# Splitting the output projection's weights a quarter earlier and reloading them, and loosening the last local attention, in a two-layer decoder trunk

## The chip, the cores and the metric

The kernel runs on one core of a Trainium2 chip (trn2). The metric is device time in microseconds from launch to end; three runs of the kernel before gave a median of 2974.0 us. A difference of less than 0.2%, some 6 us, cannot be told from no change here.

## The reference

The program is a decoder trunk of two layers over 2048 tokens of width 1024, all in float32. Layer A is a gated MLP. Layer B projects queries and a gate `z`, runs three groups of banded attention that share one key/value projection, mixes the groups by softmax of their log-sums, gates, and projects out. Cut to what matters here:

```python
DILATED_GROUPS = ((128, 1), (512, 4), (2048, 16))      # (window, dilation): groups 0, 1, 2
def dilated_layer(x, c, kv_groups, ada_w, ada_b, norm_g, w_in, q_norm_g, w_out):
    shift, scale, gate = ada_mod(c, ada_w, ada_b, 3)
    h = rms_norm(x, norm_g) * (1 + scale) + shift
    qz = h @ w_in
    q, z = ...                                          # 24 heads of 128, then 1024 columns
    for g, (window, d) in enumerate(DILATED_GROUPS):
        o, lse = dilated_group_attn(q[:, :, hs], kb, vb, slopes[hs], window, d)
    alpha = jax.nn.softmax(jnp.stack(lses), axis=0)
    o = jnp.sum(alpha[..., None] * jnp.stack(outs), axis=0)
    y = o.reshape(bsz, s, B_WIDTH) * jax.nn.silu(z)
    return x + gate * (y @ w_out)                       # w_out is b_w_out: 1024 x 1024
```

A large product takes three TensorE passes: each operand is split in a high part, rounded to the fast float32 format, and a low part, the rest. The products are high by high, high by low and low by high. ScalarE makes the high part (a copy) and VectorE the low part (a subtraction).

## The kernel before

**Stages.** The 2048 tokens are worked in four quarters of 512. In each, `layer_A` computes v, u and z of the MLP and its output product; `proj_B` then computes keys and values (`kv_block`), the queries of the three groups (`q_block`) and the gate (`z_block`). A `q_block` or `z_block` is seven products of 24 matmuls (a seven-product scheme on 2 x 2 blocks, `dense_s`). `attend` works an attention group in units of one block of 128 tokens and half of the heads. Each unit has four steps, `att_1` (transposes of keys and queries), `att_2` (scores, maximum, exponentials), `att_3` (transposes of the probabilities) and `att_4` (the product with the values, and the store).

**Fillers.** Side work is written as generators in the list `fillers`. After every few matmuls a dense stage calls `tick`, and `fill` takes the next step of each filler in turn. `rate[0]` says how many steps a tick takes. `drain` runs what is left. All loads and stores go through the SP queue, in order.

**Order on an engine.** A scheduler turns the program into one list for each engine; the engines run their lists strictly in order. A load that waits for its buffer therefore holds all loads behind it on SP.

**Rings.** Buffers come from pools: `rp` (6 raw weight tiles of 128x512), `wp` (8 split weight tiles of high and low part), `xp` (4 tiles of 128x1024; in the last stage the keys and values of a unit are in it), `tp` (8 sums), `ap` (2 of each attention tile, so two of the probabilities `pr`) and `big` (6 tiles of 16 KB on each partition).

**The last stage, `finish`.** It is started ahead of the last quarter's `z_block`. `w_out(0)` and `w_out(1)` are a filler there: 16 loads of `b_w_out` (256 KB each, L1237), each split by ScalarE (L1239) and VectorE (L1240) into four `big` tiles. The filler `first` makes the mixing weights of the first 12 tiles, loads tile 0's two attention outputs and gate with `load(0)` (L1278, L1280; three tiles of `wp`) and combines them (`prepare`). After `z_block`, for each of the 16 token tiles, `make_yb` transposes the gated sum (L1312) and splits it (L1314, L1315), and 2 x 24 matmuls give the output (L1352 to L1354). I call 24 of these matmuls a half. Meanwhile the filler `last` runs the last quarter's local attention (groups 1 and 0 of token blocks 12 to 15, `attend_local`).

**Steps of `attend`.** At iteration i, unit i is in `att_1`, unit i-1 in `att_2` and, with `skew` 1, unit i-2 in `att_3` and unit i-3 in `att_4`. With `skew` 2 the last two come a unit later. Where a stage does not exist yet (the first iterations), the generator yields only if `wrap` is set; without it the first units' steps follow each other with no step between them.

Of the kernel before, what the change touches and what calls it, by code (L numbers as in the profile page):

```python
# [34 lines left out]
def trunk(ctx, tc, out, x, c, a_ada_w, a_ada_b, a_norm_g, a_w_in, a_sgu_g, a_w_spatial,  # L35
# [29 lines left out]
    gd = dp.tile([2, D], F32, name="gd")  # L65
    hd = dp.tile([2, P, KT, 256], F32, name="hd")
# [154 lines left out]
    def ada_gate(w, b, i, nm):  # L221
        for h in range(2):
# [4 lines left out]
            nc.sync.dma_start(row, b[:, 2 * D + h * 512:2 * D + (h + 1) * 512])  # L227
            pg = pst(f"pg_{nm}{h}")
# [149 lines left out]
    flip = [False]  # L378

# [3 lines left out]
    def dense_s(ops, b, nm, evac):  # L383
# [10 lines left out]
        def product(pts, a, w, first):  # L394
# [416 lines left out]
    def layer_A(Q, hA, m, sqv, j0):  # L811
        if Q:
# [100 lines left out]
    def proj_B(Q, hk, hb, keep, rest, ahead):  # L913
# [73 lines left out]
        if Q < NQ - 1:  # L987
            drain()
            ahead()
        q_block(1)  # L990
# [192 lines left out]
    def attend_local(Q, wrap=False):  # L1183

        bs = range(4 * Q, 4 * Q + 4)
        yield from attend([(1, b) for b in bs], wrap, 0, 1 + wrap)
# [4 lines left out]
        yield from attend([(0, b) for b in bs], wrap, 3, 1 + wrap)  # L1191

    def attend(blocks, wrap=False, lead=0, skew=1):


        us = [{"id": (g, b, kh), "wrap": wrap and geom(g, b)[1] == 2, "alt": wrap and kh == 1}
# [12 lines left out]
        for i in range(len(us) + 2 + skew):  # L1209
            for k, st in ((2 + skew, att_4), (1 + skew, att_3), (1, att_2), (0, att_1)):  # L1210
# [7 lines left out]
                elif wrap or i >= len(us):  # L1218
# [11 lines left out]
    def finish():  # L1230
        wo = {}

        def w_out(n):
            wh, wl = wo[n] = [big.tile([P, KT, 512], F32R, tag="big", name=f"wo{n}{i}") for i in range(2)]
            for kk in range(KT):
                raw = rp.tile([P, 512], F32, tag="raw", name=f"rawo{n}{kk}")
                nc.sync.dma_start(raw, b_w_out[kk * P:(kk + 1) * P, n * 512:(n + 1) * 512])  # L1237
                yield
                nc.scalar.activation(wh[:, kk, :], raw, AF.Copy)  # L1239
                nc.vector.tensor_tensor(wl[:, kk, :], raw, wh[:, kk, :].bitcast(F32), ALU.subtract)  # L1240
                yield

# [30 lines left out]
        def load(t):  # L1273
            rw = slice(t * P, (t + 1) * P)
            og = {}
            for g in (0, 2):
                og[g] = wp.tile([P, D], F32, tag="w", name=f"og{t}_{g}")
                nc.sync.dma_start(og[g], od[g][rw, :])  # L1278
            og["z"] = wp.tile([P, D], F32, tag="w", name=f"zt{t}")
# [144 lines left out]
```

## Time and profile before

| what | value |
|---|---|
| median of three runs (lowest, highest) | 2974.0 us (2972.7, 2979.1) |
| profiled execution, its own time | 2975.7 us |
| its span, first to last instruction | 2973.7 us |
| mean granted TensorE clock | 0.997 |
| TensorE (PE) busy | 98% of the span |
| VectorE (DVE), ScalarE (ACT), GpSimd (POOL) busy | 71%, 56%, 25% |
| DMA | 596 MB, 200 GB/s in the mean |
| last quarter's `z_block` | 2641.9 to 2689.6 us |
| local attention and output tiles | 2692 to 2969 us |

In the profile, PE is the matmul engine, PEld the load of its stationary operand, SP the queue that issues the DMAs. A row of the timeline has the start, the time from the first start to the last end, the engine, line, operation, tiles and count; in brackets stands the idle time of the engine ahead of the row and what ended it. A row of the waits has who waited, for whom, the total in us, how often, and the longest. A row of the windows has the stretch and its length, and then the busy time of PE, PEld, DVE, ACT and POOL in it, the granted clock, the DMA engines' busy share and GB/s.

### The profile page before, as it was taken

The numbers are of one execution on the slowest core, as the hardware profiler recorded it, in microseconds if no ns is written. First come the engines' busy times: TensorE is split into PE (matmuls) and PEld (weight loads), VectorE is DVE, ScalarE is ACT, GpSimd is POOL, SyncE is SP. The second block draws the span as 40 slices with busy tenths as digits, with TensorE's granted clock in tenths as the row PEclk, the third lists the DMA queues.
The fourth block names the chain that finished last, engine by engine and source line by source line (L and its number), as shares of the span: only waits on it lengthen the run. The fifth ranks groups of instructions, "written<-read, shape, count | busy, mean of one in ns | idle before, by whom it ended". The sixth has DMA issues, their size and how long they took to land. (4 is left out here: it accounts for less than half of the span.)

```text
span 2973.7 us, 45555 instructions
## 1 busy us (share of the span) xinstructions
PE 2922.2 (98%) x14752; PEld 2446.6 (82%) x14752; DVE 2114.8 (71%) x3794; ACT 1652.1 (56%) x3386; POOL 751.2 (25%) x1044
## 2 busy tenths in 40 slices
PE   7999999999999999999999999999999999999999
PEld 5888788878888888888888888888888888977887
DVE  6877676788556676877758676877668667878772
ACT  4323355766565365776546366675555457867440
POOL 1057002320002313502315214403314220122322
PEclk9999999999999999999999999999999999999999
DMA  8899975886344466884334466873333476788642
GB/s 280 275 306 341 310 237 179 261 301 203 123 125 125 131 196 203 280 271 128 110 115 132 139 196 210 298 243 107 115 117 122 137 228 193 230 285 289 221 162 92
DMA packets 368450, 596.08 MB, mean 200 GB/s; under 512 B 39018, under 2 KB 138572, under 8 KB 368212
## 3 DMA queue, kind: packets, MB, share of 16 engines
q1 hardware_dynamic: 368212, 593.17, 61.8%
q8 instruction: 117, 1.92, 0.3%
q14 instruction: 121, 0.99, 0.1%
HBM read 472.84 MB, written 120.20 MB: 199 GB/s over the span
## 5 line engine op out<-in xcount | busy, mean ns | idle before, releaser
L276 PE MATMUL pd_o<-w_o,yh 128*128 128x512 f32 x1024 | 324.8, 397 | 3.0 <-DVE w_o L248 3.0
L276 PE MATMUL pd_kv<-w_kv,hkh 128*128 128x512 f32 x768 | 239.3, 393 | 0.3
L276 PEld LDWEIGHTS pd_o<-w_o,yh 128*128 128x128 f32 x1024 | 187.7, 189 | 40.8 <-DVE w_o L248 4.2
L314 PE MATMUL pd_u<-hAh,w_u 128*128 128x512 f32 x512 | 208.0, 406 | 0.0
L314 PE MATMUL pd_z<-hAh,w_z 128*128 128x512 f32 x512 | 203.8, 398 | 0.0
L276 PE MATMUL pd_o<-w_o,yl 128*128 128x512 f32 x512 | 200.9, 393 | 0.0
L316 PE MATMUL pd_u<-hAh,w_u 128*128 128x512 f32 x512 | 200.6, 392 | 0.0
L316 PE MATMUL pd_z<-hAh,w_z 128*128 128x512 f32 x512 | 200.1, 391 | 0.0
L315 PE MATMUL pd_u<-hAl,w_u 128*128 128x512 f32 x512 | 199.7, 390 | 0.0
L315 PE MATMUL pd_z<-hAl,w_z 128*128 128x512 f32 x512 | 199.4, 389 | 0.0
L247 ACT ACTIVATE w_u<-raw_u 128x512 fp32r<-128x512 f32 x128 | 79.8, 629 | 166.9 <-PE pd_u L316 93.0
L247 ACT ACTIVATE w_z<-raw_z 128x512 fp32r<-128x512 f32 x128 | 80.3, 631 | 160.0 <-PE pd_z L316 74.5
L276 PEld LDWEIGHTS pd_kv<-w_kv,hkh 128*128 128x128 f32 x768 | 143.2, 189 | 30.7 <-ACT hkh L566 2.0
L248 DVE TENSOR_TENSOR w_z<-raw_z,w_z 128x512 fp32r<-128x512 f32 x128 | 108.2, 853 | 80.9 <-ACT w_z L247 80.4
L1174 PEld LDWEIGHTS po<-kv,pT 128*128 128x128 f32 x1200 | 148.1, 191 | 9.1 <-ACT pT L1019 2.2
L1174 PE MATMUL po<-kv,pT 128*128 128x128 f32 x1200 | 150.6, 275 | 1.2 <-ACT pT L1019 1.2
L247 ACT ACTIVATE w_o<-raw_o 128x512 fp32r<-128x512 f32 x128 | 79.4, 628 | 129.9 <-PE pd_o L276 92.2
L276 PE MATMUL pd_kv<-w_kv,hkl 128*128 128x512 f32 x384 | 149.5, 391 | 0.0
L1113 ACT ACTIVATE pr<-pr,stat,rt 128x256 f32<-128x256 f32 (+1 forms) x224 | 123.0, 551 | 31.1 <-DVE stat L1107 15.5
L248 DVE TENSOR_TENSOR w_o<-raw_o,w_o 128x512 fp32r<-128x512 f32 x128 | 94.7, 749 | 39.5 <-ACT w_o L247 38.2
L248 DVE TENSOR_TENSOR w_u<-raw_u,w_u 128x512 fp32r<-128x512 f32 x128 | 94.0, 749 | 34.0 <-ACT w_u L247 32.1
L248 DVE TENSOR_TENSOR w_q<-raw_q,w_q 128x512 fp32r<-128x512 f32 x144 | 96.9, 693 | 24.0 <-ACT w_q L247 22.9
(826 smaller groups left out, 8030.3 us busy)
## 6 DMA issues: line engine op xcount, KB each, us to landing
raw_q<-in_b_w_in_dram SPq DMA_DIRECT2D x144, 256.0 KB, 3.6
raw_u<-in_a_w_in_dram SPq DMA_DIRECT2D x128, 256.0 KB, 3.7
raw_z<-in_a_w_in_dram SPq DMA_DIRECT2D x128, 256.0 KB, 2.9
raw_o<-in_a_w_out_dram SPq DMA_DIRECT2D x128, 256.0 KB, 3.1
qt<-qd SPq DMA_DIRECT2D x96, 260.0 KB, 3.1
raw_v<-in_a_w_in_dram SPq DMA_DIRECT2D x96, 256.0 KB, 4.2
raw_kv<-in_w_kv_dram SPq DMA_DIRECT2D x96, 256.0 KB, 2.9
od<-ot SPq DMA_DIRECT2D x96, 256.0 KB, 2.7
```

The lines of the kernel that those rows point to most:

```text
L247: nc.scalar.activation(hi, src, AF.Copy)
L248: nc.vector.tensor_tensor(lo, src, hi.bitcast(F32), ALU.subtract)
L276: last_mm[0] = nc.tensor.matmul(pt, a, u[:, w, :], start=f, stop=e, skip_group_check=more)
L314: nc.tensor.matmul(pts[i], wh, hh[:, k, :], start=k == 0, stop=False)
L315: nc.tensor.matmul(pts[i], wh, hl[:, k, :], start=False, stop=False)
L316: nc.tensor.matmul(pts[i], wl, hh[:, k, :], start=False, stop=k == KT - 1)
L1113: nc.scalar.activation(pr[:, i, :], pr[:, i, :], AF.Exp, bias=mneg[:, i:i + 1], scale=u["rt"][:, h:h + 1], accum_out=lsum[:, i:i + 1])
L1174: nc.tensor.matmul(po[:, h * P:(h + 1) * P], u["pT"][h // hp][:, h % hp, j, :], u["kv"][:, j, kh, 1, :], start=j == 0, stop=j == nk - 1)
```

## The change

It has five parts.

1. **Split earlier.** A new filler, `presplit`, runs in `layer_A` of the third quarter (`Q == 2`), whose rate goes from 2.2 to 2.6. It loads the 16 tiles of `b_w_out`, splits them in `wp` tiles and stores both parts (512 KB each) in a new DRAM tensor `wod`.
2. **Reload.** In the last quarter `load_wo` loads eight pieces of 1 MB from `wod` into four `big` tiles, from a list `jobs` that is worked off one entry at the end of each product of `dense_s`: four in `q_block(1)` and `q_block(0)`, four in the last three products of `z_block`. The filler `w_out` is gone, and the rate in `z_block` falls from 4.8 to 2.0.
3. **Last local attention.** It has `skew` 2 instead of 1, and the probabilities of every second unit are in `tp` (`alt`), as the wrapped attentions had them. The rate is 5.0 instead of 4.9.
4. **Empty first steps.** `attend` now always yields where a stage does not exist yet; this holds for group 2's attention in the last quarter too, whose rate stays 9.2.
5. **Small ones.** Tile 0's three loads go to `xp` instead of `wp`; `ada_gate` yields twice more ahead of its matmul.

```diff
+    def presplit():
+        us, raws = {}, {}
+        for i in range(2 * KT + 2):
+            if i >= 2:
+                nc.sync.dma_start(wod[(i - 2) // KT, (i - 2) % KT], us.pop(i - 2).bitcast(F32))
+            if i < 2 * KT:
+                n, kk = divmod(i, KT)
+                raws[i] = rp.tile([P, 512], F32, tag="raw", name=f"rawo{n}{kk}")
+                nc.sync.dma_start(raws[i], b_w_out[kk * P:(kk + 1) * P, n * 512:(n + 1) * 512])
+            if 1 <= i <= 2 * KT:
+                us[i - 1] = wp.tile([P, 2, 512], F32R, tag="w", name=f"wos{i - 1}")
+                split(us[i - 1][:, 0, :], us[i - 1][:, 1, :], raws.pop(i - 1))
+            yield
+
+    def load_wo(n, q):
+        if q % 2 == 0:
+            wo[n, q // 2] = big.tile([P, 4, 2, 512], F32R, tag="big", name=f"wo{n}{q // 2}")
+        h = q % 2 * 2
+        nc.sync.dma_start(wo[n, q // 2][:, h:h + 2].bitcast(F32), wod[n, 2 * q:2 * q + 2].rearrange("k p t c -> p k t c"))
...
+            job = jobs.pop(0) if jobs else None
+            if job:
+                with tc.issue_after(last_ld[0].ins):
+                    job()
...
-            rate[0] = 2.45 if Q == 1 else 2.2
+            rate[0] = 2.45 if Q == 1 else 2.6 if Q == 2 else 2.2
...
+            if Q == 2:
+                fillers.append(presplit())
...
+        if Q == NQ - 1:
+            for n in range(2):
+                jobs.extend([None] * 2 + [lambda n=n: load_wo(0, 2 * n), None, None, lambda n=n: load_wo(0, 2 * n + 1), None])
+            jobs.extend([None] * 4 + [lambda: (load_wo(1, 0), load_wo(1, 1)), lambda: load_wo(1, 2),
+                                      lambda: load_wo(1, 3)])
...
-        yield from attend([(1, b) for b in bs], wrap, 0, 1 + wrap)
+        yield from attend([(1, b) for b in bs], wrap, 0, 1 + (wrap or alt), wrap or alt)
...
-        yield from attend([(0, b) for b in bs], wrap, 3, 1 + wrap)
+        yield from attend([(0, b) for b in bs], wrap, 3, 1 + (wrap or alt), wrap or alt)
...
-                elif wrap or i >= len(us):
+                else:
                     yield
...
+            pool, tag = (wp, "w") if t else (xp, "xin")
...
-            yield from attend_local(NQ - 1)
+            yield from attend_local(NQ - 1, False, True)
...
-        fillers.extend([fs, both()])
-        rate[0] = 4.8
+        fillers.append(fs)
+        rate[0] = 2.0
...
-        rate[0] = 4.9
+        rate[0] = 5.0
```

No matmul, VectorE or GpSimd instruction is added or taken away over the whole program, and ScalarE loses seven table loads. What is new are the 16 stores and the 8 reloads. The rest is order.

**SP in the last three products of the last `z_block`.** `raw_z3bt` from `wt_0` are the weights of the fifth product, those from `wt_3` of the sixth, `raw_z3b` those of the seventh; `rawo` is a piece of `b_w_out`, `wo` a reload, `zd` a store of the gate. Before:

```order
L255 DMA raw_z3bt_3_26126<-wt_0_116 128x512
L960 DMA qd_92<-st_q30u_25254 128x520
...
L1237 DMA rawo_26140<-in_b_w_out_dram 128x512
L1237 DMA rawo_26158<-in_b_w_out_dram 128x512
...
L255 DMA raw_z3bt_0_26179<-wt_3_119 128x512
...
L969 DMA zd<-zb_2_26172 128x512
L255 DMA raw_z3bt_3_26194<-wt_3_119 128x512
...
L1237 DMA rawo_26212<-in_b_w_out_dram 128x512
...
L255 DMA raw_z3b_0_26243<-in_b_w_in_dram 128x512
...
L255 DMA raw_z3b_3_26258<-in_b_w_in_dram 128x512
L1237 DMA rawo_26268<-in_b_w_out_dram 128x512
...
L969 DMA zd<-zb_2_26236 128x512
```

After:

```order
L258 DMA raw_z3bt_3_26201<-wt_0_117 128x512
...
L258 DMA raw_z3bt_0_26243<-wt_3_120 128x512
...
L258 DMA raw_z3bt_3_26258<-wt_3_120 128x512
L403 DMA wo_26231<-wod 128x2x1024
L1000 DMA zd<-zb_0_26118 128x512
...
L403 DMA wo_26231<-wod 128x2x1024
L403 DMA wo_26286<-wod 128x2x1024
L258 DMA raw_z3b_0_26299<-in_b_w_in_dram 128x512
L1000 DMA zd<-zb_2_26236 128x512
...
L258 DMA raw_z3b_1_26304<-in_b_w_in_dram 128x512
...
L258 DMA raw_z3b_3_26314<-in_b_w_in_dram 128x512
L403 DMA wo_26286<-wod 128x2x1024
```

The weights of the fifth and sixth product now stand ahead of any gate store; three reloads of 1 MB and two pairs of gate stores stand ahead of the seventh product's last three pieces.

**PE at the start of the last local attention.** `pyb` are the transposes of tile 0, `pf` its output, `pk` and `pq` the transposes of `att_1`, `ps` the scores of `att_2`, `pp` the transposes of `att_3`. Before, with only some of the output matmuls shown:

```order
L1312 MATMUL pyb_0_26317<-ident,og_0_25973 128x128 x4
...
L1050 MATMUL pk_12_26370<-ident,kv_12_26363 128x128 x4
L1352 MATMUL pf_0_26356<-wo_25883,yb_26316 128x512
...
L1060 MATMUL pq_12_0_26378<-ident,qt_12_0_26366 128x128 x4
L1352 MATMUL pf_1_26497<-wo_26156,yb_26316 128x512
...
L1098 MATMUL ps_12_00_26391<-kT_12_26375,qT_12_0_26383 128x256
```

After:

```order
L1337 MATMUL pyb_0_26358<-ident,og_0_26094 128x128 x4
...
L1086 MATMUL pk_12_26420<-ident,kv_12_26401 128x128 x3
L1373 MATMUL pf_0_26397<-wo_24371,yb_26357 128x512
...
L1096 MATMUL pq_12_0_26428<-ident,qt_12_0_26404 128x128 x2
...
L1373 MATMUL pf_1_26453<-wo_26231,yb_26357 128x512
...
L1337 MATMUL pyb_0_26455<-ident,og_0_26351 128x128 x4
...
L1134 MATMUL ps_12_00_26492<-kT_12_26425,qT_12_0_26433 128x256
```

Between the first unit's `pq` and its `ps` stood 16 output matmuls before; now its scores come in the second half, behind the rest of the first half and the transposes of tile 1 (the second `pyb`), and its `pp` follow in the fourth half instead of the second. The last `po` (the `att_4` product) of the local attention moves from half 16 of 32 to half 20.

More of the change, by code (lines that the diff above doesn't have):

```diff
@@ L65, in trunk @@
     gd = dp.tile([2, D], F32, name="gd")
+    wod = dp.tile([2, KT, P, 2, 512], F32, name="wod")
     hd = dp.tile([2, P, KT, 256], F32, name="hd")
@@ L227, in ada_gate @@
             nc.sync.dma_start(row, b[:, 2 * D + h * 512:2 * D + (h + 1) * 512])
+            yield
+            yield
             pg = pst(f"pg_{nm}{h}")
@@ L1230, in finish @@
     def finish():
[L1231 to L1241, printed above, removed]
         gb = [bcast(gd[1:2, n * 512:(n + 1) * 512], f"gb{n}") for n in range(2)]
@@ L1317, in finish @@
         fs = first()
-        def both():
-            yield from w_out(0)
-            yield from w_out(1)
-        fillers.extend([fs, both()])
-        rate[0] = 4.8
+        fillers.append(fs)
+        rate[0] = 2.0
         yield
```

20 lines of the change are left out of this document (11 added, 9 removed).

## The prediction

> **What bounds the kernel now.** I read the page's first part, then TensorE's waits by stretch of time, then the windows of those stretches.
>
> ```profile
> span 2973.7 us, 45555 instructions
> PE 2922.2 (98%) x14752; PEld 2446.6 (82%) x14752; DVE 2114.8 (71%) x3794; ACT 1652.1 (56%) x3386; POOL 751.2 (25%) x1044
> ```
>
> PE is busy for all but 51.5 us of its span. The change adds and removes no matmul, so it can win no more than the part of these idle times, and of the slow matmuls beside them, that lies where it reorders. The waits of PE in three stretches (group 2's attention in the last quarter; the last `z_block`; the output tiles) say where that is:
>
> ```profile
> PE pp L1155 <- ACT pr L1113: 3.1, 1, 3.1
> PE po L1174 <- ACT pT L1019: 1.2, 2, 0.7
> PE pq L1060 <- DMA qt<-qd: 1.2, 1, 1.2
> PE pp L1155 <- DVE b_s L1103: 0.5, 1, 0.5
> PE pk L1050 <- DVE pr L1103: 0.4, 1, 0.4
> ...
> PE pd_z3bb L276 <- DVE w_z3b L248: 2.1, 2, 1.2
> PE pd_z3ba L276 <- ACT w_z3bt L247: 1.8, 1, 1.8
> PE pf L1352 <- ACT yb L1314: 1.3, 1, 1.3
> ...
> PE pp L1155 <- ACT pr L1113: 3.8, 3, 1.4
> PE ps L1098 <- ACT qT L1065: 2.9, 1, 2.9
> PE pyb L1312 <- DVE pT L1017: 0.3, 1, 0.3
> ```
>
> In `z_block` PE waits for split weights, in the attentions for probabilities. The windows give what each stretch loses; the fourth is the `z_block` of the quarter before, which has no `b_w_out` beside it:
>
> ```profile
> 100.00:400.00 300.00, 297.24 (x1396) 248.69 (x1395) 214.01 (x276) 100.39 (x179) 101.92 (x72) 0.99 0.93 311
> 1357.00:1434.00 77.00, 77.00 (x434) 66.59 (x433) 54.62 (x108) 42.74 (x84) 23.53 (x37) 1.00 0.36 112
> 1890.30:1931.30 41.00, 41.00 (x193) 33.88 (x192) 33.30 (x50) 24.10 (x41) 16.96 (x22) 1.00 0.89 303
> 2450.00:2470.00 20.00, 15.55 (x82) 12.30 (x81) 8.02 (x25) 8.24 (x24) 3.33 (x7) 0.91 0.44 142
> 2465.00:2642.00 177.00, 174.49 (x1141) 155.14 (x1142) 141.89 (x359) 147.48 (x413) 26.46 (x55) 0.99 0.74 231
> 2641.90:2689.60 47.70, 41.73 (x169) 32.11 (x168) 34.91 (x54) 29.29 (x53) 8.81 (x15) 0.96 0.87 293
> 2780.00:2800.00 20.00, 17.10 (x85) 14.57 (x84) 10.05 (x19) 5.45 (x14) 4.93 (x3) 0.91 0.79 268
> 2692.00:2880.00 188.00, 180.39 (x1138) 157.69 (x1139) 151.49 (x304) 107.69 (x306) 58.92 (x36) 0.99 0.64 217
> ```
>
> **The change part by part.** I sum against the profiled execution's own 2975.7 us.
>
> *The last `z_block`.* Two products of the timeline, one behind the other, give the length of an undisturbed one:
>
> ```profile
> 2636.46 5.60 PE L276 MATMUL pd_q30a<-w_q,hob 128*128 128x512 f32 x24
> 2641.90 5.60 PE L276 MATMUL pd_z3bb<-w_z3b,hob 128*128 128x512 f32 x24
> ```
>
> Starts are 5.44 us apart, so seven products need 38.1; this `z_block` took 47.7 and lost 9.6. What goes away is 16 loads in the six raw tiles that the z weights use too, and their splits:
>
> ```profile
> L1239 ACT ACTIVATE wo<-rawo x16: 614/631/634, 2637.3 to 2690.7; 128x512 fp32r<-128x512 f32 x16
> L1240 DVE TENSOR_TENSOR wo<-rawo,wo x16: 677/685/693, 2640.9 to 2691.3; 128x512 fp32r<-128x512 f32 x16
> DMA to landing us min/median/max: 3.7/4.6/5.5
> ```
>
> That is 10 us of ACT and 11 of DVE. The z weights get the six raw tiles for themselves, and wp too, since tile 0 now lies in xp. That such a block can run without loss at 303 GB/s the window 1890 to 1931 shows. What stays is the seventh product. The reloads wait on SP until PE is done with the third and fourth product (their `big` tiles hold its operands), and behind them stand gate stores and the seventh product's weights, then tile 1's loads. Three reloads of 1.05 MB at this window's 293 GB/s take 10.7 us; from the third product's end to the seventh's start are 3 x 5.44 = 16.3; the 5.6 left are a load's landing (4.6) and one pair of splits (1.3), just too few. The seventh product waited before too:
>
> ```profile
> 2684.48 5.28 PE L276 MATMUL pd_z3bb<-w_z3b,hob 128*128 128x512 f32 x22 [0.93 <-DVE w_z3b L248]
> ```
>
> Now its third piece stands on ACT behind the sixth's two gate activations. I leave 1.6 us lost: **-8.0**, between -9.6 and -2.6 (all four pieces late, by a landing and splits).
>
> *First output matmul.* ACT came to `yb` behind the last `b_w_out` splits, and PE waited 1.3. One gate activation still stands ahead of each half of `yb`, at about the 0.63 us of the copy above: **-0.7** (0 to -1.3). What is late next is tile 1: its gate load stands on SP behind the last gate stores. From the seventh product's end these need two sums (0.7 each) and two activations (0.6), then a landing of 4.6 and POOL's product of 2.4 (its row stands below), 9.6 us; PE has the first half and four matmuls, 6.3, the transposes and the wait ahead of them, 2: **+1** (0 to +3).
>
> *Last local attention.* PE lost 7.0 us in waits, and 20 x (1 - 0.91) = 1.8 us by the slower clock behind the longest (the window from 2780). `ps` gets most of a half more cover behind `pq`, against 2.9 us of wait; `pp` gets a whole unit's work more behind its exponentials, against waits of 1.4 at most. DVE's work there (151 us of 188) is the same, over four more halves. Its `pr` in `tp` adds two buffers to the two that had to come free. Some first-unit waits will stay: **-6.0** (0 to -8.8; a loss is left to the rivals).
>
> *Group 2's attention* gets the same empty steps. PE lost 6.4 us in waits (the first five rows; 0.7 of it in the last units) and 1.8 us of clock (window from 2450). The 1.2 for `qt` should go, since the second unit's `pq` comes 12 kv matmuls behind the first's instead of 4. The way from the scores to the probabilities was 8.5 us, from the end of
>
> ```profile
> 2455.34 1.16 PE L1094 MATMUL ps<-kT,qT 128*128 128x128 f32 x8
> ```
>
> to 2465.0, and PE had 5.4 us of work or waits in between; the new order puts 18 kv matmuls (5.44 / 24 = 0.227 us each, 4.1) and some 2 us of transposes and scores there. 2 us of waits stay and half of the clock: **-3.5** (0 to -7.5).
>
> The clock is seen in the rows of the two longest waits:
>
> ```profile
> 2465.01 0.95 PE L1155 MATMUL pp<-ident,pr 128*128 128x128 f32 x2 [3.10 <-ACT pr L1113]
> 2465.62 1.20 PE L276 MATMUL pd_kv<-w_kv,hkh 128*128 128x512 f32 x2
> 2793.18 0.58 PE L1098 MATMUL ps<-kT,qT 128*128 128x256 f32 x1 [2.90 <-ACT qT L1065]
> 2793.56 0.41 PE L1099 MATMUL ps<-kT,qT 128*128 128x256 f32 x1
> ```
>
> Two matmuls of 512 columns take 1.20 us behind the wait of 3.10. [...]
>
> *Price in the q-blocks.* Four reloads of 1.05 MB stand on SP between query loads. VectorE runs in order and already waits there:
>
> ```profile
> DVE rt L1070 <- DMA qt<-qd: 18.9, 17, 3.1
> ```
>
> With 141.9 busy of 177 it has 16 us left over. Four reloads hold what is behind them by up to 1.05 / 293 = 3.6 us each, 14 in all, so the slack would just bear it: **+2** (0 to +8, half of it passed on).
>
> *Price in the third quarter.* 16 x (0.26 + 0.52) MB more over the first 36 filler steps; at 2.6 steps a tick, with two ticks to a block of 48 matmuls (10.9 us), that is some 76 us and 166 GB/s on top of 112, 278 in all. From 100 to 400 us PE kept 99% at 311 GB/s. ACT and DVE get 10 and 11 us in 77, where they were busy for 43 and 55, while attention steps are halved for that time. A split product pair there lasts 12 x 0.227 = 2.7 us; with three wp tiles lent out five remain, 13.6 us ahead, three landings. **+1** (0 to +28, the rival below).
>
> *`ada_gate`.* This wait in the first quarter goes, and the steps behind it shift a little: **-0.6**.
>
> ```profile
> PE pg_ga L229 <- DVE acc_ga L178: 0.8, 1, 0.8
> ```
>
> *End of the local attention.* It moves from half 16 to 20 of 32, towards tile 12, which needs its result. From the last sums to the end of a tile's product on POOL the chain was 10.3 us, and a tile lasts 11.77:
>
> ```profile
> 2867.78 1.23 DVE L1170 TENSOR_TENSOR stat<-stat,stat 128x4 f32<-128x4 f32 x1
> 2875.72 2.41 POOL L1290 TENSOR_TENSOR og<-og,zt 128x1024 f32<-128x1024 f32 x1 [6.73 <-PE pf L1354]
> 2940.06 1.09 ACT L1314 ACTIVATE yb<-pyb 128x512 fp32r<-128x512 f32 x2 [10.69 <-PE pyb L1312]
> 2951.83 1.09 ACT L1314 ACTIVATE yb<-pyb 128x512 fp32r<-128x512 f32 x2 [10.69 <-PE pyb L1312]
> ```
>
> Half 24, where tile 12 is transposed, begins three halves (17 us) behind half 20. Cost 0; with the chain twice as long it would be 3 us.
>
> Sum: -8.0 - 0.7 + 1 - 6.0 - 3.5 + 2 + 1 - 0.6 = -14.8, to 2960.9. The profiled execution was 1.7 us above the median, so **2959 us** as a median; its own range is 2953 to 2966.
>
> **Rivals.**
>
> - *All of it goes.* For: the other `z_block` has no loss. Against: first units always wait for something. 9.6 + 1.3 + 8.8 + 7.5 + 0.8 = 28.0 less: 2946.
> - *The reloads starve the seventh product and the query loads.* 293 GB/s speak for it, the z weights now standing ahead of the reloads against. `z_block` wins 2.6 and the q-blocks lose 5 where I have 8.0 and 2: 8.4 more, 2967.
> - *The waits for probabilities stay*, since VectorE sets the chain's pace, and its work stays:
>
> ```profile
> 2692.00:2740.00 48.00, 45.94 (x300) 40.41 (x301) 44.60 (x78) 38.24 (x107) 18.35 (x8) 1.00 0.85 294
> ```
>
> 93% busy speaks for it; against it that fewer units now stand in these halves. Local attention wins 1.0, group 2's nothing: 8.5 more, 2968.
> - *Slower: the loss of the `z_block` moves to the third quarter and grows.* The same 16 loads share the same six raw tiles, now with 16 stores of twice the size that wait on SP for their split, ahead of the u weights. In `z_block` a load cost 9.6 / 16 = 0.6 us; with the stores at 1.2 it is 16 x 1.8 = 28.8, less the 1 I have: 2987. It decides once a u weight lands later than the 13.6 us for which split tiles are there. Against: 4.6 us of landing at 293 GB/s.
> - *No net change*, where half of the gains are kept and 8 us are paid: 2974.
>
> **Chances.** Forecast 0.45, all gone 0.08, reloads starve 0.15, waits stay 0.12, slower 0.12, none 0.08. A median within 0.2% (6 us, 2968 to 2980) is no change that a measurement can tell. Of the two middling rivals, at the bound, a third falls there, so faster is 0.45 + 0.08 + 0.10 + 0.08 = 0.71, no change 0.17, slower 0.12. The range reaches up to 2974, which leaves out the slower case and half of none, and down to 2948, which leaves out most of the first rival.
>
> **What would show it.** In the new profile: no wait of PE for z weights but in the seventh product, and `z_block` within 40 us; one wait under 1 us at the first output matmul; less than 3 us of waits from there on, and no window at 0.91; in the third quarter's u stretch PE still at 100% with some 270 GB/s; query waits of VectorE above 19 us but none of PE. I am wrong if PE waits for u weights, if it waits for `wo`, or if tile 12's transposes wait for POOL.

## The result and the profile after

The changed kernel is slower. Nine runs gave a median of 2982.9 us (2981.6 to 2989.4), nine of the kernel before 2975.7 (2971.0 to 2979.1). The ratio of the runs is 1.0033, with a 95% interval of 1.0024 to 1.0043: 7 to 13 us more, some 9.8 of 2974. The prediction said 2959. One profiled execution of the experiments below, that of e14, ran at a granted clock of 0.66 and took 4186 us, so for e14 there is the ratio of its other runs and no stage lengths.

The profiled execution took 2982.0 us, 6.3 more than that of before. The first part of its page:

```profile
span 2979.8 us, 45570 instructions
PE 2921.9 (98%) x14752; PEld 2448.6 (82%) x14752; DVE 2115.6 (71%) x3794; ACT 1643.3 (55%) x3379; POOL 757.2 (25%) x1044
```

Every engine is as busy as before. PE stood idle for 57.9 us instead of 51.5. So the question is again where it waits. I cut both timelines of PE at the first matmul of a stage (the first that writes the named tile) and compared the lengths:

| stage (from, to) | before, us | change, us | predicted, us |
|---|---|---|---|
| start to the first quarter's queries (`pd_q02a`) | 461.4 | +5.1 | -0.6 |
| second quarter, `layer_A` and keys (`pd_v1a` to `pd_q12a`) | 462.8 | +1.5 | 0 |
| third quarter, the same (`pd_v2a` to `pd_q22a`) | 473.2 | +4.1 | +1 |
| last quarter, the same (`pd_v3a` to `pd_q32a`) | 473.3 | +1.7 | 0 |
| last query blocks with group 2 (`pd_q32a` to `pd_z3bb`) | 237.3 | 0.0 | -3.5 + 2 |
| last `z_block`, to the first `pf` | 50.5 | -10.1 | -8.0 - 0.7 |
| output tiles, first to last `pf` | 275.8 | +3.8 | +1 - 6.0 |

The other stages (query and gate products of the first three quarters, 178.0 us each) are the same to 0.1. The terms add up to the 6.1 us between the spans. The gain in `z_block` is there and larger than forecast. It is eaten by stages that the prediction had at about nothing.

The waits of PE name what stands there. First the kernel before, between 300 and 700 us:

```profile
PE pd_o L276 <- DVE w_o L248: 2.8, 1, 2.8
...
PE pt_b L560 <- DVE xr L893: 0.5, 1, 0.5
```

The kernel after, in the same stretch:

```profile
PE pt_b L589 <- DVE xr L924: 5.4, 1, 5.4
...
```

The kernel after from 2460 to 2700 us (group 2 and `z_block`), and from 2692 (the output tiles):

```profile
PE pq L1096 <- DMA qt<-qd: 3.8, 1, 3.8
...
PE pd_z3bb L279 <- DVE w_z3b L251: 0.2, 1, 0.2
...
PE ps L1134 <- DVE yb L1340: 2.7, 2, 1.7
PE pyb L1337 <- POOL og L1315: 2.1, 1, 2.1
PE ps L1136 <- DVE qT L1102: 2.0, 2, 1.1
PE pf L1375 <- DVE yb L1340: 1.8, 1, 1.8
PE ps L1134 <- DVE kT L1092: 1.4, 1, 1.4
...
```

All waits of `pp` for `pr` are gone, as forecast: 3.1 us in group 2 and 3.8 in the output tiles. In group 2 a wait of 3.8 for a query load stands in their place. In the output tiles it is VectorE's queue, with 7.9 us, and tile 1's gate, with 2.1.

**The first quarter.** The two `yield`s in `ada_gate` push all later steps of its side work. SP's rows of the kernel before:

```profile
390.39 0.32 SPq L360 DMA_DIRECT2D wt<-st_cw  x1
...
403.77 0.93 SPq L890 DMA_DIRECT2D x1d<-xr  x2
```

Its last store of combined weights (`wt`) goes out at 390.4. The kernel after, the rows of SP, VectorE and PE:

```profile
392.72 8.21 SPq L363 DMA_DIRECT2D wt<-st_cw  x8
401.02 3.66 SPq L258 DMA_DIRECT2D raw_kv<-in_w_kv_dram  x6
404.77 0.85 SPq L921 DMA_DIRECT2D x1d<-xr  x2
411.52 0.75 DVE L924 TENSOR_SCALAR xr<-xr,r_b 128x1024 f32<-128x1024 f32 x1 [2.46 <-DMA x1d<-xr]
412.42 1.09 PE L589 MATMUL pt_b<-ident,xr 128*128 128x128 f32 x4 [5.37 <-DVE xr L924]
```

Now eight such stores (256 KB each) and six loads of key weights stand right ahead of the store of the rows `xr`. VectorE may scale these rows in place only when that store has read them. It does so 6.8 us after the store's issue at 404.8; in the kernel before it was 3.1 us (403.77 to 406.83). PE, which transposes the rows next, waits 5.4 us.

**The third quarter.** Its `u` stretch, where `presplit` loads and stores, costs nothing: PE 77.00 of 77 us at 259 GB/s. The loss lies in the output product, two stages later. Windows of the kernel after, the `u` stretch and two of the output product (columns as in the prediction):

```profile
1363.00:1440.00 77.00, 77.00 (x410) 66.00 (x409) 54.67 (x98) 42.08 (x80) 12.94 (x20) 1.00 0.77 259
...
1600.00:1657.00 57.00, 55.77 (x324) 47.90 (x324) 50.28 (x118) 24.54 (x65) 34.24 (x42) 1.00 0.47 148
1657.00:1718.00 61.00, 59.56 (x311) 49.59 (x310) 39.47 (x80) 22.32 (x52) 18.23 (x24) 1.00 0.45 143
```

The same two of the kernel before:

```profile
1593.00:1650.00 57.00, 57.00 (x324) 49.09 (x323) 47.08 (x106) 29.52 (x66) 28.28 (x37) 1.00 0.40 125
1650.00:1707.00 57.00, 57.00 (x291) 47.83 (x290) 33.94 (x64) 18.96 (x42) 13.02 (x17) 1.00 0.50 160
```

In `u` GpSimd, which works for the attention, has 12.9 us instead of 23.5 (the prediction shows that window). In the output product GpSimd and VectorE have 11 and 9 us more than before, in windows that are 4 us longer. Some of the attention that `presplit` displaced runs there, beside the splits of `w_o`.

### The profile page after: what moved, and what is told of

It is laid out like the page before. It is cut to its first block, busy times and chain, and to the rows that moved or that the text cites. A ratio compares the mean times of both kernels' runs of the same rounds, so it can differ in the third digit from the quotient of the medians.

```text
span 2979.8 us, 45570 instructions
## 1 busy us (share of the span) xinstructions
PE 2921.9 (98%) x14752; PEld 2448.6 (82%) x14752; DVE 2115.6 (71%) x3794; ACT 1643.3 (55%) x3379; POOL 757.2 (25%) x1044
## 5 line engine op out<-in xcount | busy, mean ns | idle before, releaser
L1149 ACT ACTIVATE pr<-pr,stat,rt 128x256 f32<-128x256 f32 (+1 forms) x192 | 104.2, 545 | 40.1 <-DVE stat L1143 23.4
L250 ACT ACTIVATE w_q<-raw_q 128x512 fp32r<-128x512 f32 x144 | 88.6, 626 | 46.8 <-PE pd_kv L279 11.2
```

The costliest lines, as they stand in the source:

```text
L250: nc.scalar.activation(hi, src, AF.Copy)
L1149: nc.scalar.activation(pr[:, i, :], pr[:, i, :], AF.Exp, bias=mneg[:, i:i + 1], scale=u["rt"][:, h:h + 1], accum_out=lsum[:, i:i + 1])
```

## The experiments

Each kernel was timed in five rounds beside the kernel before. The columns behind the ratio are the stage lengths of its profiled execution against those of before, as above: the first quarter, the third quarter, the last quarter's `layer_A`, group 2, `z_block`, output tiles.

| run | ratio | interval | 1st | 3rd | last A | grp 2 | z | tiles |
|---|---|---|---|---|---|---|---|---|
| the change | 1.0033 | 1.0024–1.0043 | +5.1 | +4.1 | +1.7 | 0.0 | -10.1 | +3.8 |
| e1 yields alone | 1.0023 | 1.0014–1.0032 | +4.5 | -0.9 | -0.3 | -1.1 | +3.2 | -1.1 |
| e2 change, no yields | 1.0007 | 0.9997–1.0017 | -3.0 | +4.8 | +2.1 | +0.9 | -9.9 | +9.7 |
| e3 change, old local attention | 1.0043 | 1.0031–1.0056 | +2.5 | +4.9 | +2.5 | +0.9 | -10.1 | +6.1 |
| e4 change, old group 2 | 1.0040 | 1.0025–1.0054 | +4.2 | +5.2 | +2.5 | +1.1 | -8.4 | +4.4 |
| e5 split, reload, xp | 1.0010 | 0.9999–1.0021 | +0.5 | +4.2 | +1.6 | -0.8 | -7.2 | +3.2 |
| e6 both attentions alone | 0.9997 | 0.9988–1.0006 | -3.0 | -0.4 | -0.2 | +1.3 | -1.1 | +1.4 |
| e7 e2, tile 0 in wp | 1.0036 | 1.0023–1.0049 | -2.8 | +3.3 | +1.0 | -0.2 | +1.8 | +0.5 |
| e8 presplit alone | 1.0034 | 1.0020–1.0047 | -0.9 | +7.0 | +2.3 | +0.3 | +1.1 | +2.6 |
| e9 tile 0 in xp alone | 0.9991 | 0.9982–1.0001 | -1.5 | +1.8 | +0.5 | +1.0 | -3.3 | +1.3 |
| e10 e9 and attentions | 0.9995 | 0.9984–1.0005 | -2.9 | +0.7 | 0.0 | -2.6 | -0.7 | +0.9 |
| e11 e2, rate 3.8 | 0.9990 | 0.9979–1.0001 | -1.4 | +2.9 | -0.3 | +4.1 | -8.7 | +6.4 |
| e12 e2, tile rate 4.4 | 0.9992 | 0.9981–1.0003 | -0.3 | +7.6 | +1.0 | -0.4 | -9.6 | +1.2 |
| e13 e11 and e12 | 0.9981 | 0.9973–0.9990 | -2.9 | +2.2 | -0.5 | +0.6 | -9.0 | +1.5 |
| e14 e13, tile rate 4.0 | 0.9979 | 0.9969–0.9989 | | | | | | |
| e15 e13, old group 2 | 0.9977 | 0.9968–0.9986 | -2.4 | +2.2 | -0.2 | +2.6 | -6.5 | -2.7 |
| e16 e13, old local attention | 0.9989 | 0.9978–0.9999 | -0.6 | +3.5 | -0.1 | +1.1 | -8.6 | +3.9 |
| e17 e2, gate on VectorE | 0.9999 | 0.9988–1.0010 | -2.0 | +8.8 | +1.7 | +0.1 | -3.2 | -7.3 |
| e18 e15, gate on VectorE | 0.9968 | 0.9955–0.9980 | -2.4 | +3.7 | -0.1 | +1.8 | -8.7 | -5.3 |

Stage lengths are of one execution each. The first quarter has the same steps in all kernels without the yields, and there they lie between -3.0 and +0.5; so a single difference under some 3 us says little, a column that repeats says more. A profiled execution need not be a typical one either: that of e2 took 4.5 us more than the median of e2's runs and that of e11 7.7 more, that of e7 7.8 less and that of e13 4.6 less. Where the ratio and the stage lengths disagree, the ratio decides.

**The yields (e1, e2).** Alone in the kernel before, and taken out of the change:

```diff
             nc.sync.dma_start(row, b[:, 2 * D + h * 512:2 * D + (h + 1) * 512])
+            yield
+            yield
             pg = pst(f"pg_{nm}{h}")
```

> The kernel before, with only the two added yields in ada_gate. Theory A (the profile after shows 5.4 us of PE waiting for the scaled rows in the first quarter, behind weight stores that came some 7 us later): the yields alone cost 4 to 7 us, 2980 to 2982 where the kernel before has 2975, and the wait of pt_b for xr near 412 us stands in this profile too. Rival B (the wait is scatter of one execution, or comes from elsewhere in the change): within 2 us of the kernel before, pt_b waits under 1.5 us in all up to 1280 us.

> The changed kernel without the two yields in ada_gate. Theory A: 5 to 7 us less than the changed kernel, 2976 to 2978, and kv_block(0) of the first quarter starts where it did in the kernel before (415 us). Rival B: no change, 2983.

Alone they cost 0.23%, 6.8 us. Without them the change goes from 1.0033 to 1.0007, 7.7 us less, and the two intervals don't touch. Neither leaves room for the -0.6 of the prediction. The mechanism is in e1's rows, the same as in the kernel after:

```profile
391.98 8.62 SPq L362 DMA_DIRECT2D wt<-st_cw  x8
...
403.59 0.86 SPq L892 DMA_DIRECT2D x1d<-xr  x2
...
410.95 1.09 PE L562 MATMUL pt_b<-ident,xr 128*128 128x128 f32 x4 [5.26 <-DVE xr L895]
```

In the three profiles of the change with yields (the kernel after, e3, e4) this wait was 5.4, 4.7 and 5.7 us; in e2 it was 0.5.

**The orders of the attentions (e3, e4, e6).** e3 takes the new order out of the last local attention (with its old rate 4.9), e4 takes the empty first steps out of group 2, e6 puts both attentions' parts alone into the kernel before. The edit of e3 in part; `pad` is a new argument, false for an attention without the empty steps:

```diff
-            yield from attend_local(NQ - 1, False, True)
+            yield from attend_local(NQ - 1)
...
-                else:
+                elif pad or wrap or i >= len(us):
                     yield
```

> The changed kernel with the last local attention as before (skew 1, no probabilities in tp, no empty first steps there, rate 4.9); group 2 keeps its empty steps. Theory A (the new order of the local attention itself costs time, since its transposed keys and queries now stand behind the split of yb on VectorE): 3 to 6 us less than the changed kernel, 2977 to 2980, with waits of pp for pr again and none of ps for yb. Rival B (the tail is long because tile 1 comes late and VectorE is held beside GpSimd, whatever the order): within 1.5 us of the changed kernel. The prediction's own reason (the new order saves 6 us): 6 us more, 2989.

> The changed kernel without the empty first steps in group 2's attention; the local attention keeps its own. Theory A (a wait for the query load took the place of the wait for probabilities): within 1.5 us of the changed kernel, 2982 to 2984, with a wait of pp for pr of some 3 us and none for qt over 2 us. The prediction's reason (the empty steps save 3.5 us): 2 to 5 us more. Rival (the empty steps bring the third query load behind the stores of the keys and values and so cost more than they save): 2 to 4 us less.

> The kernel before with the new order of the attentions alone: skew 2, probabilities in tp and rate 5.0 in the last local attention, empty first steps in both; b_w_out is loaded and split in the last z_block as before. The prediction's terms (-6.0 - 3.5): 7 to 10 us less than the kernel before. Theory A (the local attention wins 3 us as e3 told, group 2 wins 0 to 2): 3 to 5 us less. Rival B (the waits of the output tiles for yb and qT come with this order, whatever the z_block does): 0 to 4 us more, with ps waiting for yb in this profile.

e3 is 0.10% above the change, some 3 us, and e4 0.07%, some 2, each with intervals that overlap. e6 is 0.9997 (-3.6 to +1.8 us): the 9.5 us that the prediction gave to the two orders aren't there. My theory that the new local order itself costs time fell with e3, which is not faster. In e3 the old waits of `pp` for `pr` are back (7.4 us, 2.5 twice), beside one of 1.35 for `yb`: each order has its own kind of wait. In e6 `ps` waits 3.9 us for `yb`, so that wait comes with the new order, with or without the reload. For group 2 the trace of the kernel after shows what came in the place of the wait for probabilities:

```profile
2466.70 0.32 SPq L1075 DMA_DIRECT2D qt<-qd  x1
2472.84 2.25 SPq L956 DMA_DIRECT2D kvd<-hs_k  x4
2475.18 0.45 SPq L1075 DMA_DIRECT2D qt<-qd  x1
...
2478.55 1.09 PE L1096 MATMUL pq<-ident,qt 128*128 128x128 f32 x4 [3.79 <-DMA qt<-qd]
```

The third unit's query load stands on SP behind the stores of the normalised keys (`kvd`), which wait for VectorE until 2472.8. The kernel after asks for that load with the third unit's step, but PE reaches this step before the stores are out. All eleven profiles with the empty steps in group 2 have one such wait for `qt`, 3.0 to 4.1 us, and none of `pp` for `pr`. Of the eight without them five have the wait of 3.1 for `pr`; e4, e5 and e8 have neither, at about the same length of the stage (+1.1, -0.8, +0.3).

**What of the z_block's gain is whose (e5, e7, e9, e10).** e5 has only the split, the reload, tile 0 in `xp` and the rates. e7 is e2 with tile 0 in `wp`; e9 is the kernel before with tile 0 in `xp`; e10 adds both attentions to e9. The edit of e9:

```diff
         def load(t):
+            pool, tag = (wp, "w") if t else (xp, "xin")
...
-                og[g] = wp.tile([P, D], F32, tag="w", name=f"og{t}_{g}")
+                og[g] = pool.tile([P, D], F32, tag=tag, name=f"og{t}_{g}")
...
```

> The changed kernel without the two yields and with both attentions as before: what is left of the change is the split in the third quarter, the reload, tile 0 in xp and the rates 2.6 and 2.0. Theory A (the z_block's gain of some 10 us is kept, 4 us go in the third quarter, 2 in the last quarter's layer A and 6 in the output tiles): within 0.1% of the kernel before, 2970 to 2975 where that has 2972. Rival B (the output tiles lose time by the new order of the attention alone): 4 to 7 us less than the kernel before. The prediction's own terms (-8.0 - 0.7 + 1 + 2 + 1): 5 us less.

> The changed kernel without the two yields and with tile 0's three loads in wp as before. Theory A (what the output tiles lose comes from tile 1's late gate and from VectorE, not from xp): z_block loses 2 to 5 us more by the three wp tiles, the output tiles stay within 1.5 us of e2; 2 to 5 us more than e2. Rival B (tile 0 in xp keeps the keys of the local attention waiting and costs the output tiles 4 us or more): 2 to 4 us less than e2.

> The kernel before with one edit: tile 0's three loads go to xp instead of wp. Theory A (e7 showed that with tile 0 in wp the z_block loses all again, so the three wp tiles and not the loads of b_w_out were what it lost by): the z_block takes 5 to 10 us less, the output tiles give 2 to 4 back, 2 to 7 us less in all. Rival B (the 16 loads and splits of b_w_out in the raw tiles were the loss, as the prediction said): z_block within 2 us, total within 2 us.

> The kernel before with tile 0 in xp and the new order of both attentions; no split a quarter earlier, no reload, no yields. Theory A: as e9, with the output tiles 0 to 2 us better or worse, 2 to 7 us less than the kernel before. Rival B (what the z_block wins the output tiles lose, since VectorE sets their pace): z_block 5 to 10 us less, output tiles 5 to 10 us more, within 2 us of the kernel before.

Neither part does it alone. The reload without `xp` leaves the `z_block` at +1.8 (e7), `xp` without the reload at -3.3 and -0.7 (e9, e10); with both it is -6.5 to -10.1 in eleven of the twelve profiles (e17, with the gate's product moved too, is the other, -3.2). In time e7 lies 0.29% above e2, 8.6 us, for one line on tile 0. Both theories of e9 were too simple. Not all that `z_block` wins stays won: e7's output tiles took 9 us less than e2's in these profiles, and why is not traced. The rows of e7 show why the reload alone doesn't help:

```profile
2659.45 0.43 SPq L401 DMA_DIRECT2D wo<-wod  x1
...
2661.76 0.87 SPq L401 DMA_DIRECT2D wo<-wod  x1
2662.73 3.77 SPq L256 DMA_DIRECT2D raw_z3bt<-wt  x4
...
2674.51 5.72 PE L277 MATMUL pd_z3ba<-w_z3bt,hob 128*128 128x512 f32 x14 [5.56 <-ACT w_z3bt L248]
```

With three split tiles lent to tile 0, the sixth product's weights come behind two reloads of 1 MB on SP, and PE waits 5.6 us. In the kernel after they stand ahead of the reloads, as the front part's rows show, and the window of its whole `z_block` has only 0.2 us without work at 349 GB/s:

```profile
2654.30:2693.30 39.00, 38.77 (x170) 31.26 (x169) 27.39 (x41) 22.07 (x41) 9.13 (x14) 1.00 0.98 349
```

**The third quarter (e8, e11).** e8 is the kernel before with `presplit` and its rate; it stores weights that nothing reads. e11 is e2 with a higher rate while `presplit` runs:

```diff
-            rate[0] = 2.45 if Q == 1 else 2.6 if Q == 2 else 2.2
+            rate[0] = 2.45 if Q == 1 else 3.8 if Q == 2 else 2.2
...
             yield
+        rate[0] = 2.2
```

> The kernel before with the 16 loads, splits and stores of presplit and the rate 2.6 added in the third quarter; the stored weights are never read, b_w_out is loaded and split again in the last z_block. Theory A: 4 to 6 us more than the kernel before, of which 3.5 to 5 between the third quarter's v and its first query block and 1.5 to 2.5 in the last quarter's layer A. The prediction's term: 1 us more. Rival (the loss of the z_block moves here whole): 28 us more.

> The changed kernel without the yields (e2), with rate 3.8 while presplit runs and 2.2 behind it, so that the attention beside it loses 3 steps instead of 12 and is not pushed into the output product of the third quarter. Theory A (the 4 us of the third quarter are attention work that moved beside the splits of w_o): 2 to 4 us less than e2 there, and w_o waits under 1 us. Rival B (the loads and stores themselves, 350 GB/s then): PE waits for u weights and the third quarter takes 2 us or more longer than in e2.

`presplit` alone costs 0.34%, 10 us, in time; its profile has 9.3 of it in the third quarter and the last quarter's `layer_A`, 2.8 of these in the `v` product, ahead of `presplit`. Over all nine profiles with the rate 2.6 the third quarter lost 3.3 to 8.8, over the four without `presplit` -0.9 to +1.8, over the five with 3.8 then 2.2 it lost 2.2 to 3.7. From the first `u` matmul on, where `presplit` begins, the three groups stand clear of each other: 4.2 to 6.5, 0.0 to 0.5, and 1.5 to 2.2. The last quarter's `layer_A` lost 1.0 to 2.5 with 2.6 and nothing with 3.8. In time e11 is 0.17% below e2, with intervals that just overlap. The waits in the third quarter's output product of the kernel after, between 1590 and 1720 us:

```profile
PE pd_o L279 <- DVE w_o L251: 1.2, 2, 1.1
...
```

and of e13, which has the rate 3.8 too:

```profile
PE pd_o L277 <- DVE w_o L249: 0.3, 1, 0.3
```

The transfers are the same at both rates, so more than half of the price in the third quarter comes from the attention steps that `presplit` took the place of, and not from the transfers. PE's waits in these 130 us come to 2.6 of the 4.1 us, 1.4 of them for split weights; the rest of it, the 1.5 to 2.2 us that stay at rate 3.8, and the loss in the last quarter are not traced.

**The output tiles (e12 to e16).** e12 to e14 change one number, the rate over the output tiles, e12 on top of e2, e13 and e14 on top of e11. e15 and e16 are e13 with group 2, or the last local attention, in its old order. The edit of e12:

```diff
-        rate[0] = 5.0
+        rate[0] = 4.4
```

> The changed kernel without the yields (e2), with rate 4.4 instead of 5.0 over the output tiles. Theory A (VectorE and its sharing with GpSimd set the pace of the first 20 halves): spreading the same work over 23 halves makes the waits of ps for yb, kT and qT smaller, 2 to 5 us less than e2. Rival B (tile 1's late gate and single late loads): within 1.5 us of e2. Rival C (the local attention then ends too late for tile 12): 3 us or more longer.

> The changed kernel without the yields, with rate 3.8 beside presplit (as e11) and 4.4 over the output tiles (as e12). Theory A (two separate prices, each from work pushed too densely into one stretch): the gains add, 0.2 to 0.35% less than the kernel before, 2965 to 2969 where that has 2974; the output tiles within 3 us of the kernel before. Rival B (e11 and e12 are scatter around e2): 0 to 0.1% more than the kernel before.

> As e13, but with rate 4.0 over the output tiles, so that the local attention is spread over some 25 halves. Theory A (density on VectorE makes the waits): the waits of PE between the first output matmul and half 20 fall again, but the attention ends at tile 12; within 2 us of e13 or up to 3 us less. Rival C (tile 12 then waits for it): 2 to 6 us more than e13, with one wait of pyb near 2880 us. Rival B (single late loads): within 1 us of e13.

> As e13, without the empty first steps in group 2's attention. Theory A (a wait for the query load took the place of that for probabilities, nothing won): within 2 us of e13, with the wait of pq for qt under 2.5 us. The prediction's reason: 2 to 5 us more than e13. Rival (the third query load behind the stores of keys and values costs more than the empty steps save): 2 to 4 us less.

> As e13, with the last local attention in the old order (skew 1, no probabilities in tp, no empty steps there) at the same rate 4.4. Theory A (the new order saves some 2 to 3 us of waits for probabilities as e3 told): 2 to 4 us more than e13. The prediction's reason: 6 us more. Rival B (density alone decides): within 1.5 us of e13.

With 4.4 the output tiles took 1.2 us more than before (e12) where e2's took 9.7 more. PE's waits for VectorE there fell from 8.7 us (e2) to 4.2 (e12). e12 is 0.15% under e2 in time and e13 0.09% under e11; each pair overlaps, but both go one way, and so do the stage lengths. e13 is the first kernel clearly faster than that before, 0.9981. e14 adds nothing and loses nothing: tile 12 did not come to wait by a measurable amount. e15 equals e13 within its interval (0.9977 against 0.9981): group 2's empty steps are worth nothing that can be measured, either way. e16 lies 0.08% above e13, with intervals that overlap: if the new local order is worth anything it is some 2 us, a third of the 6 forecast.

**What holds VectorE (e17, e18).** In the output tiles of the kernel after some of VectorE's instructions take much longer than their like. Rows of VectorE, GpSimd and PE:

```profile
2719.47 3.31 POOL L1315 TENSOR_TENSOR og<-og,zt 128x1024 f32<-128x1024 f32 x1 [3.92 <-DVE stat L1143]
2720.63 3.23 DVE L1314 TENSOR_TENSOR og<-og,og 128x1024 f32<-128x1024 f32 x1
2724.00 2.36 POOL L1315 TENSOR_TENSOR og<-og,zt 128x1024 f32<-128x1024 f32 x1 [1.22 <-DMA xr<-x1d]
2724.99 1.41 DVE L1106 COPY rt<-qt 128x8 f32<-128x8 f32 x1
2725.21 0.35 PE L1134 MATMUL ps<-kT,qT 128*128 128x256 f32 x1 [1.40 <-DVE kT L1092]
...
2751.79 2.37 POOL L1315 TENSOR_TENSOR og<-og,zt 128x1024 f32<-128x1024 f32 x1 [6.00 <-DVE stat L1143]
2752.16 2.03 DVE L1106 COPY rt<-qt 128x8 f32<-128x8 f32 x1
2754.84 0.38 PE L1134 MATMUL ps<-kT,qT 128*128 128x256 f32 x1 [1.72 <-DVE yb L1340]
```

The copy of eight numbers a row has a median of 0.165 us in this stage; here it takes 2.03 and 1.41. Both times it ends together with the GpSimd product that was running (2754.19 against 2754.16, 2726.40 against 2726.36), and what stands behind it on VectorE is what PE then waits for. The sum of 3.23 us runs 2.15 until GpSimd's product ends at 2722.78 and 1.08 behind that; a like sum at 2718.12 takes 1.21 in all. I took these three rows as VectorE being held by GpSimd's product, which they suggest but don't prove; e17 and e18 move the product:

```diff
-            nc.gpsimd.tensor_tensor(y, y, og["z"], ALU.mult)
+            nc.vector.tensor_tensor(y, y, og["z"], ALU.mult)
```

> The changed kernel without the yields (e2), with the product of the combined attention and the gate on VectorE instead of GpSimd. In the changed kernel's profile three VectorE instructions (3.2, 2.0 and 1.4 us instead of 1.2 and 0.15) end together with that GpSimd product, and PE waits for what stands behind them. Theory A (VectorE is held by GpSimd's product): VectorE gets 16 x 1.2 us more work and loses the holds; no copy of rt over 0.3 us, PE's waits for kT, qT and yb fall by 3 to 6 us, tile 1 comes 1 us earlier; 2 to 5 us less than e2. Rival (VectorE is simply too full): 2 to 6 us more than e2.

> As e15 (no yields, rate 3.8 beside presplit, 4.4 over the output tiles, group 2 as before), with the gate's product on VectorE. Theory A: 1 to 3 us less than e15, since at 4.4 VectorE has room. Rival: 1 to 4 us more.

The output tiles become 17 us shorter than e2's (-7.3 against +9.7). Windows of the whole stage, e2 and then e17:

```profile
2685.80:2971.20 285.40, 273.46 (x1556) 236.86 (x1557) 182.88 (x336) 120.45 (x335) 89.16 (x54) 0.97 0.56 189
2696.40:2964.80 268.40, 265.67 (x1556) 230.43 (x1557) 190.86 (x351) 119.61 (x335) 51.07 (x39) 1.00 0.59 199
```

VectorE gets 15 more sums of 1.21 us here, 18 us, but is busy for only 8.0 us more; the 10 between them are my estimate of what it was held. From e15 to e18 it is the same, 5.6 us for 18 of work. Not every long copy is gone: in e17 one of `rt` still takes 0.85 us, against the 0.3 that the expectation allowed. PE's idle time falls by 9 us, and up to 8 more are the clock, 0.97 over 285 us in e2 and 1.00 in e17. e17's waits of PE from 2680 us on are three, the first of them in `z_block`:

```profile
PE pd_z3bb L277 <- ACT w_z3b L248: 4.7, 1, 4.7
PE ps L1132 <- DVE yb L1338: 2.2, 2, 1.4
PE ps L1134 <- DVE qT L1100: 0.5, 2, 0.3
```

In time e17 is only 0.08% under e2, some 2 us, with intervals that overlap. So the 17 us are of these two executions; e2's had a granted clock of 0.97 in this stage, and it was e2's slowest. At the lower rate the longest waits that e18 has left over the output tiles are these:

```profile
PE pp L1190 <- DVE yb L1339: 1.3, 1, 1.3
PE pyb L1336 <- DVE pT L1052: 0.9, 1, 0.9
PE pp L1190 <- ACT st_pr L1148: 0.4, 1, 0.4
...
```

e18 is the fastest kernel of the study: 0.9968 of the kernel before (0.9955 to 0.9980), 6 to 13 us less, and some 19 less than the change as it was made. Against e15, from which it differs by the gate's product alone, it is 0.09% faster, 2.7 us, and the intervals overlap: the rows show copies on VectorE of 2.03 and 1.41 us, against a median of 0.165, that end with GpSimd's product; what they cost in time is not clear of the scatter.

## Why the prediction was wrong

*The sum.* It gave -14.8 us, the profile +6.1. By stage the 21 us between them are: first and second quarter 7.2, third quarter and last `layer_A` 4.8, group 2 with the reloads 1.5, output tiles 8.8, less 1.4 that `z_block` did better.

*`ada_gate`* (-0.6) failed as a step, and it is one of the two largest errors: +6.8 alone. The prediction named a wait of 0.8 us (`pg_ga`) that would go away and wrote that the steps behind it "shift a little". The wait did not go: it is 1.7 us in the kernel after and 0.7 in e1. And the prediction did not ask past which queue the steps shift. The side work's eight stores moved on SP to right ahead of the store of `xr`, whose end VectorE and then PE wait for. Neither the sum nor any rival had this.

*The last `z_block`* (-8.0, with -0.7 for the first output matmul) held: -10.1, one wait of 0.2 us in the seventh product, none at the first output matmul. Its reason was only half right. The loads of `b_w_out` in the raw tiles counted, but without the line on tile 0, which the prediction named in half a sentence, nothing was won (e7).

*Tile 1's late gate* (+1) held in kind and was sized too small: PE waited 2.1 us for its product on GpSimd (3.2 in e2).

*The last local attention* (-6.0): the waits of `pp` and of `ps` for ScalarE went, as said. The step that failed is "DVE's work there (151 us of 188) is the same, over four more halves", used as a reason that VectorE would not be late: the new order puts the transposed keys and queries behind VectorE's other work, with instructions of 1.41 to 3.23 us beside GpSimd's products, and PE waited 7.9 us for VectorE. The stage lost 3.8 us instead of winning 5. The order is not all of it, for the changed kernel loses here with the old order too (e3 +6.1, e5 +3.2, with 7.4 and 5.9 us of waits for `pr` where the kernel before had 3.8). In time the order is worth 2 to 3 us (e3, e16), the rate some 4 (e12) and the gate's product 2 to 3 (e17, e18); none of these is clear of the scatter by itself, all go one way.

*Group 2* (-3.5, and +2 for the reloads): nothing changed, 0.0. The wait for probabilities was replaced by one of 3.8 us for the third query load. The prediction had looked at the second unit's load only. The reloads cost PE nothing that the profile shows: the first goes out at 2490 us, behind that wait, and no wait of PE over 0.8 follows until the output tiles; VectorE's waits for queries over this stage went from 28.6 to 24.1 us, so the +2 was not there.

*The third quarter* (+1) failed, though its own evidence was right: PE stayed at 100% in `u` at 259 GB/s, near the 278 worked out. The prediction wrote that the "attention steps are halved for that time" and used this as room. It did not follow the displaced steps to where they run, up to the output product, where PE then waited for split weights (1.4 us, none before). The price with the last quarter's `layer_A` was 5.8 us here and 9.3 in e8, more than half of it gone at the other rate (e11, e13).

*The rivals.* "All gone" was true of `z_block` alone. "The reloads starve the seventh product" is near to what e7 shows (the sixth product waits 5.6 us there, the seventh 2.0), not the change. "The waits for probabilities stay" is wrong in its words and right in its reason, VectorE's pace. The slower case named one of the quarters that lost, by the wrong mechanism: no `u` weight was late. The 0.12 for slower was too small for a change that moves work past queues in four stages that had no idle time to give.

*The clock.* The 3.8 us wait in group 2 left the granted clock at 0.91 over 2470 to 2490, as the prediction had read it behind the longest waits before.

*The signs.* `z_block` without waits but in the seventh product, PE at 100% in `u`, and no wait at tile 12 came as named. Missed were "less than 3 us of waits" in the output tiles (10.9 us idle there), "no window at 0.91" (2720 to 2740 has it) and no query wait of PE (3.8). One reading slips: of the windows shown, the `z_block` of the quarter before is the third, not the fourth; the argument uses the right one.

What stays open: how much of the output tiles' loss comes from VectorE's long instructions beside GpSimd's products and how much from its load (e17 and e18 move both), why the stage loses with the old order too, why the last quarter's `layer_A` depends on the rate of the quarter before, and single differences of 2 to 3 us, which lie within the scatter.

## What to carry to other kernels

A step that is delayed need cost nothing by itself; ask which queue it is moved past, and what now stands behind it there. Work put into an idle stretch pushes the work that ran there into a later one: follow it to the stretch where it ends up, and price it by the waits of that stretch. Before spreading VectorE's work, look for its instructions that take several times their median, and at what GpSimd runs beside them.

## What was unexpected of the hardware

The clock of the kernel after fell behind short waits too. PE waited 1.40 and 0.95 us within 3 us, and matmuls behind them took 0.41 us instead of the 0.28 of one at 2725.40:

```profile
2727.10 0.39 PE L1136 MATMUL ps<-kT,qT 128*128 128x256 f32 x1 [0.95 <-DVE qT L1102]
2728.04 0.41 PE L1134 MATMUL ps<-kT,qT 128*128 128x256 f32 x1
```

The windows of the stretch with these waits and of the next, and of a later pair with one wait of 1.72 us in its first:

```profile
2724.10:2727.50 3.40, 1.34 (x8) 1.13 (x9) 3.40 (x5) 0.11 (x1) 3.40 (x2) 1.00 0.19 72
2727.50:2730.90 3.40, 3.40 (x18) 3.40 (x18) 3.05 (x9) 0.88 (x2) 0.09 (x1) 0.50 0.74 207
...
2751.30:2754.80 3.50, 1.82 (x13) 1.25 (x10) 3.50 (x6) 3.13 (x10) 3.01 (x2) 1.00 0.68 267
2754.80:2758.20 3.40, 3.36 (x23) 3.06 (x24) 3.40 (x6) 1.93 (x6) 0.60 (x1) 1.00 0.57 153
```

In the first pair PE is idle for 2.06 of 3.40 us, and the granted clock of the next 3.40 is 0.50; in the later pair it is idle for 1.68 of 3.50 us, and the clock stays at 1.00. By my estimate 3.40 us at 0.50 cost up to 1.7 us of matmuls, more than the longer of the two waits here. In e17's third quarter the clock was 0.83 over 1666 to 1676, with two waits of 1.01 and 1.06 us for `w_o` in that stretch.
